# Moving VectorE's sums and additions in the doubled products of an encoder layer's second MLP half

## The chip, the cores and the metric

One of the eight cores of a Trainium2 chip runs the whole kernel in one launch. The metric is the device time of one execution in microseconds (us); the time of a kernel is the median of its runs.

## The reference, cut to what matters

The kernel computes one layer of an encoder on a sequence of 2048 positions with 1024 features, all in float32: an attention mixer with two groups of heads, and behind it an MLP with a squared ReLU. Everything of this case lies in the MLP:

```python
h = rmsnorm(x, g_norm2[l]) * (1.0 + sc2) + sh2
x = x + gt2 * (jnp.square(jax.nn.relu(h @ w1[l])) @ w2[l])
```

`w1` is 1024 x 4096, `w2` is 4096 x 1024, `gt2` is a gate per feature.

## The kernel before, in words

**Float32 from three passes.** Every operand of a matrix product is split into a rounded high part (a cast on ScalarE) and the rest (a subtraction on VectorE, 128 x 512 elements), and TensorE multiplies high by high, high by low and low by high (`mm3`). So each operand tile costs VectorE one subtraction, and the tiles that hold the split operands (`opp`, 8 buffers) bound how far the splitting can run ahead of TensorE.

**Fewer products, more sums.** A product of 2 x 2 blocks is done with seven products in place of eight, at the price of sums of blocks ahead of it and behind it (Strassen's scheme in Winograd's form). The seven are called 1, 5, 6, 3, 7, 2, 4, in the order of `OUTER`. `column_sum` is such a sum on VectorE.

**First half of the MLP** (`First`, h @ w1). It runs for two halves of the sequence, `mb` 1 and then `mb` 0. Each has 16 rows `j` (two column blocks of `w1`), and each row has seven steps, one for each product, of 12 matmuls. Row `j` needs three sums of blocks of `w1` in tiles of their own: `First.fetch` makes sum 5 (pieces 21 and 22), sum 6 (of sum 5 and piece 11), sum 3 (of piece 12 and sum 6) and, in place, sum 7. The tiles come from `temp`, a pool of 7 buffers of 128 x 512 (`tp`). In the profile they are `ts`: `ts<-w` is sum 5, `ts<-ts,w` sum 6, `ts<-w,ts` sum 3. In the half `mb` 0 the rows 0 to 7 also take four tiles each from this pool (`other`, in the profile `to`): a block of the hidden layer of `mb` 1, loaded, subtracted from on VectorE and stored to `scr_hid` by `keep`. Behind the products, `cp` in the profile holds the sums of results; the column sum behind product 7 reads the PSUM bank that product 4 of the same row goes on adding to.

**Second half of the MLP** (hidden @ w2). Products 1 and 6 are done plainly (`Second`, 16 steps of 24 matmuls each, `plain`). The other five, 7, 5, 2, 3, 4 in this order (`DOUBLE`), are each done once more by seven products (`Outer`), for both halves of the sequence at once: 56 steps of 6 matmuls, eight steps for each of 1, 5, 6, 3, 7, 2, 4. The order at the end of the kernel is: `First` of `mb` 0 (112 steps), `plain(0, 1)`, doubled 7, `plain(0, 6)`, doubled 5, 2, 3, 4.

A step of `Outer` uses an operand of the hidden layer (`opr` in the profile, one for each step) and one of the weights (`ol`, one for two steps). Ahead of that, VectorE makes, for each doubled product:

- sums of blocks of the hidden layer, 128 x 1024 elements, four (`g` 0 to 3) of each kind (`half_sum`, `r<-r,r` in the profile): 6 from 3 and 5, 7 from 6 and 1, 4 from 2 and 6, and for doubled product 5 alone also 5 from 5 and 1. `plan["sum"]` gives for each kind the step of the first and the gap to the next; it is made one doubled product ahead. `f` is the step at which the doubled product starts, `e` that at which it ends. A sum 6 is read from step 16 of its doubled product on, a sum 7 from step 32, a sum 4 from step 48, each some five steps earlier by the splitting.
- the loads of these blocks (`half`, at the steps of `plan["load"]`).
- behind the last step of 5, 6, 3, 7, 2 and 4 (steps 15, 23, 31, 39, 47, 55) the results, weighted by the gate and added to rows of x (`weigh`, `cxo` and `txo` in the profile): four for each of them in the doubled products 7 and 5, two in 2, 3 and 4.
- in 2, 3 and 4, `update`: four more rows added (`txu` in the profile), each fetched into a tile of `temp` at a step of its first list, added at a step of its second list, and stored three steps later.

The sums of blocks of `w2` for the doubled products are made beforehand, while `First` runs, and stored to `scr_t`. `outer_sums` does it in pieces of 128 x 2 x 256 (`wt` in the profile): a load into one of four large buffers (`raw_pair`, which also hold the rows of `w1`) six steps ahead, then four sums at four steps, each stored two steps later. `narrow_sums` does the same for half as much at a time, in two tiles of `temp` (`twn`): loads four steps ahead, four sums of 128 x 256 at four steps, each stored two steps later. Before, it serves doubled product 2 in `mb` 1 only.

**What sets the order.** Nearly everything here is written out by hand: `at(n, job)` puts a job at step n, and the loop over the steps prepares operands as far ahead as 8 buffers allow, then runs the jobs of the step, then its matmuls. Each engine, and the DMA queue of SyncE (SP), runs its instructions in exactly this order. A tile of a pool is taken by whoever asks next, and the writer waits until the last user of that buffer has finished (a store: until it has landed).

Of the kernel before, what the change touches and what calls it, by code (L numbers as in the profile page):

```python
# [9 lines left out]
F32 = mybir.dt.float32  # L10
# [8 lines left out]
P = 128  # L19
# [60 lines left out]
def encoder_kernel(ctx, tc, xT, c, g1, g2, w_in, w_rest, gqk, bias, w_o, w1, w2, w_ada, b_ada, out):  # L80
    nc = tc.nc
    act, dve, pool, sp = nc.scalar, nc.vector, nc.gpsimd, nc.sync
# [156 lines left out]
    if True:  # L239
# [248 lines left out]
        act, dve, pool = (Ordered(tc, e) for e in (act, dve, pool))  # L488
# [189 lines left out]
    if True:  # L678
# [540 lines left out]
        op = ph.enter_context(tc.tile_pool(name="op", bufs=2))  # L1219
# [69 lines left out]
    HP = NP // 2  # L1289
# [6 lines left out]
    if True:  # L1296
# [5 lines left out]
        np2 = pm.enter_context(tc.tile_pool(name="np2", bufs=2, side="right"))  # L1302
# [16 lines left out]
        def column_sum(eng, out, a, b, op):  # L1319
            eng.tensor_tensor(out, a, b, op=op)  # L1320
            return out

        def temp(nm):
            return tp.tile([P, TB], F32, tag="t", name=f"t{nm}")
# [9 lines left out]
        def at(n, job):  # L1334
            jobs.setdefault(n, []).append(job)
# [120 lines left out]
        class First(Step):  # L1456
# [29 lines left out]
            def fetch(self, m=None):  # L1486
                d = self.load()
                for n in range(4) if m is None else (m,):
                    pr, a, b, op = ((5, "21", "22", ALU.add), (6, 5, "11", ALU.subtract), (3, "12", 6, ALU.subtract), (7, "11", "21", ALU.subtract))[n]
                    d[pr] = column_sum(dve, d["21"] if pr == 7 else temp(f"s{self.nm}_{pr}"), d[a], d[b], op)  # L1490
                return d

            def run(self):
# [147 lines left out]
        def update(mb, r, odd, loads, adds, home=None, last=False):  # L1641

            xs = {}

            def fetch(n):
                xs[n] = x = (home or temp)(f"xu{mb}_{r}{odd}_{n}")
                sp.dma_start(x, scr_x[2 * mb + odd, HK * r + n])

            def add(n):
                x, row = xs[n], HK * r + n  # L1650
                weigh(x, Second.whole["s", n], row)
                dst = rows_of(out, mb, row, odd) if last else scr_x[2 * mb + odd, row]
                later.add(3, lambda: sp.dma_start(dst, x))

            for n in range(HK):
                at(loads[n], lambda n=n: fetch(n))
                at(adds[n], lambda n=n: add(n))
# [10 lines left out]
        def outer_sums(i, m, step):  # L1668

            t = []  # L1670

            def load():
                t.append(raw_pair([P, 2, 2, TB], F32, f"wt{i}_{m}"))
                for a in range(2):
                    if i in (3, 7, 5):
                        sp.dma_start(t[0][:, a], scr_s[i - 1 if i < 7 else 0, HP // 2 * a + m])
                        continue
                    r, s = {2: (0, 1), 4: (1, 1)}[i]
                    j = HP * a + 2 * m
                    for q in range(2):  # L1680
                        sp.dma_start(t[0][:, a, q, :], w2[2 * (j + q) + s][:, r * TB : (r + 1) * TB])

            def sums(pr, dst, a, b, op):
                v = {nm: t[0][:, h, :, c * CN : (c + 1) * CN] for nm, h, c in (("11", 0, 0), ("12", 1, 0), ("21", 0, 1), ("22", 1, 1))}
                column_sum(dve, v[dst], v[a], v[b], op)
                later.add(2, lambda: sp.dma_start(scr_t[i, pr][:, 2 * m : 2 * m + 2, :], v[dst]))

            at(step - 6, load)
            todo = ((5, "22", "21", "22", ALU.add), (7, "21", "11", "21", ALU.subtract))
            todo += ((6, "11", "22", "11", ALU.subtract), (3, "12", "12", "11", ALU.subtract))  # L1690
            for n, x in enumerate(todo):
                at(step + n, lambda x=x: sums(*x))

        def narrow_sums(i, k, step):

            t = []
            r, s = {2: (0, 1), 4: (1, 1)}[i]

            def load():
                for a in range(2):  # L1700
                    t.append(temp(f"wn{i}_{k}_{a}"))
                    sp.dma_start(t[a], w2[2 * (HP * a + k) + s][:, r * TB : (r + 1) * TB])

            def sums(pr, dst, a, b, op):
                v = {nm: t[h][:, c * CN : (c + 1) * CN] for nm, h, c in (("11", 0, 0), ("12", 1, 0), ("21", 0, 1), ("22", 1, 1))}
                column_sum(dve, v[dst], v[a], v[b], op)
                later.add(2, lambda: sp.dma_start(scr_t[i, pr][:, k, :], v[dst]))

            at(step - 4, load)
            todo = ((5, "22", "21", "22", ALU.add), (7, "21", "11", "21", ALU.subtract))  # L1710
            todo += ((6, "11", "22", "11", ALU.subtract), (3, "12", "12", "11", ALU.subtract))
            for n, x in enumerate(todo):
                at(step + n, lambda x=x: sums(*x))
# [154 lines left out]
        for mb in (1, 0):  # L1868
            begin = len(steps)
            steps += [First(mb, j, i) for j in range(NP) for i in OUTER]  # L1870
            end = len(steps)
            for j in range(NP):
                f = steps[begin + 7 * j]
                if mb:
                    second_sums(j, begin + 7 * j + 2)
                    if j >= HP:
                        narrow_sums(2, j - HP, begin + 71 + 5 * (j - HP))
                else:
                    outer_sums((7, 5, 3, 4)[j // 4], j % 4, begin + 7 * j - 2)
                    if j < HP:  # L1880
                        for i, n in ((3, 4), (2, 5), (7, 4), (4, 5)):
                            at(begin + 7 * j + n, lambda i=i, f=f: f.other(i))
                if j > mb:
                    at(begin + max(7 * j - 13, 2 if mb else -6), f.load)
                if j > mb or mb and j:
                    for m in range(4):
                        at(begin + (m + 1 if mb and j == 1 else 7 * j - 9 + (m if j > 1 else 0)), lambda f=f, m=m: f.fetch(m))
            if mb:
                norm2(1, begin + 18)
                norm2(0, begin + 48)  # L1890
                for k in range(HK):
                    begins = end + 6 * k
                    pieces = right_blocks(0, k, kept if k % 2 else temp)
                    for n, m in ((0, 0), (4, 4), (5, 5), (6, 6), (7, 7), (8, 7), (9, 7), (10, 7), (11, 7), (12, 7)):
                        at(begins + n, pieces[m])
                for i in PLAIN:
                    plain(1, i)
                for n in range(end, len(steps), 2):
                    at(n - 7 - max(0, end + 4 - n) // 2, steps[n].load)
                rest = len(steps)  # L1900
                lent = lambda nm: rp.tile([P, TB], F32, tag="r", name=nm)
                for n, (r, odd) in enumerate(((0, 0), (1, 1), (1, 0))):
                    at_row = rest + 3 + 16 * n
                    update(1, r, odd, range(at_row, at_row + 16, 4), range(at_row + 4, at_row + 20, 4), lent)
            else:
                at(begin - 8, steps[begin].load)
                at(begin - 6, steps[begin].fetch)
# [5 lines left out]
        f = plain(0, 1)  # L1913
        plain_loads(f, [9, 9, 9, 8, 8, 8])
        e = len(steps)
        plan = {"load": {1: (f - 3, 1), 5: (f + 1, 2), 3: (f + 6, 2), 2: (f + 18, 2)}}
        plan["sum"] = {6: (f + 12, 2), 7: (f + 15, 2), 4: (f + 44, 2)}
        for i in DOUBLE:
            f = outer(i, plan)
            e = len(steps)  # L1920
            if i == 7:
                plain_loads(plain(0, 6), [12, 11, 11, 11, 9, 8])
            spread = lambda *ns: [f + n for n in ns]
            if i == 2:
                update(0, 0, 0, spread(18, 22, 26, 30), spread(24, 28, 32, 36))
                pass
            if i == 3:
                update(0, 1, 1, spread(18, 22, 26, 30), spread(24, 28, 32, 36))
            if i == 4:
                update(0, 1, 0, spread(2, 6, 10, 14), spread(8, 12, 16, 20), None, True)  # L1930
            plan = {"load": {1: (f + 22, 2), 5: (f + 17, 2), 3: (f + 30, 2), 2: (f + 46, 2)}}
            plan["sum"] = {6: ({7: e + 8, 5: e - 4}.get(i, f + 38), 2), 7: (e + (20 if i == 7 else 16), 2), 4: (e + (30 if i == 7 else 26), 2)}
            if i == 7:
                plan["sum"][5] = (e + 1, 2)

        blocks = [right_blocks(1, k, kept if k else temp) for k in range(HK)]

# [104 lines left out]
```

## Time and profile before

| | |
|---|---|
| median of 3 runs | 2557.26 us (2556.21 to 2559.08) |
| the profiled execution's own time | 2558.36 us |
| its span, first to last instruction | 2556.6 us |
| granted TensorE clock | 0.999 |
| TensorE busy | 2520.1 us (99%) |
| TensorE weight loads busy | 2095.2 us (82%) |
| VectorE busy | 2055.6 us (80%) |
| ScalarE busy | 1510.6 us (59%) |
| DMA | 714.66 MB, mean 280 GB/s |

The matmuls are pipelined, so their durations overlap, and TensorE's busy time says little; what a step costs is read from the distance between the starts of two steps. In the rows of the timeline a bracket tells how long the engine stood idle before the instruction and what ended that. Idle time of VectorE or of SP costs nothing by itself; it counts where TensorE stands behind it.

### The profile page before, as it was taken

The page shows a single profiled execution, that of the slowest core. Times are in us where ns is not written, and L with a number is a line of the kernel's source. Part 1 is how long each engine was busy: PE and PEld are TensorE (multiplying, and loading weights), DVE is VectorE, ACT ScalarE, POOL GpSimd, SP SyncE. Part 2 cuts the span into 40 slices and gives each one's busy share as a digit, 9 for nine tenths or more (in the row PEclk, how much of TensorE's full clock was granted, in tenths as well). Part 3 has the DMA queues.
Part 4 walks back from the last instruction along what each step waited for, and adds up shares of the span by engine and source line. Part 5 has one row for each costly group of instructions (what it writes and reads, how often), then busy time and mean ns, then how long its engine had stood idle before and what let it go on. Part 6 is the DMA issues. An engine that isn't in the chain of part 4 may idle for free.

```text
span 2556.6 us, 39502 instructions
## 1 busy us (share of the span) xinstructions
PE 2520.1 (99%) x12388; PEld 2095.2 (82%) x12388; DVE 2055.6 (80%) x3593; ACT 1510.6 (59%) x2893; POOL 746.0 (29%) x1128
## 2 busy tenths in 40 slices
PE   9999999999999999999999999999999999999999
PEld 7888888888888888887888888888778888887777
DVE  7656767887789878998868777789887759899998
ACT  6333425668866687666755555575455546466665
POOL 4330144776776667776610000000000000000000
PEclk9999999999999999999999999999999999999999
DMA  9879979779977788866887888996998896868884
GB/s 360 327 294 365 342 279 295 213 237 287 285 238 235 236 253 272 262 211 194 233 312 251 296 288 311 336 344 220 339 338 289 273 354 264 339 240 292 284 261 130
DMA packets 305105, 714.66 MB, mean 280 GB/s; under 512 B 32512, under 2 KB 91904, under 8 KB 293248
## 3 DMA queue, kind: packets, MB, share of 16 engines
q1 hardware_dynamic: 303600, 707.43, 80.9%
q10 hardware_dynamic: 1296, 4.72, 0.5%
q8 instruction: 98, 1.61, 0.3%
q14 instruction: 111, 0.91, 0.1%
HBM read 485.00 MB, written 227.02 MB: 279 GB/s over the span
## 4 chain that ended last, share of the span: by engine, by line
PE 74%; DVE 14%; DMA 4%; ACT 3%; issue 3%; POOL 1%; SPq 0%; DVEq 0%; ACTq 0%; POOLq 0%
PE ps L42 21%; PE ps_s L42 11%; PE pt L42 11%; PE acc L42 6%; PE wt L42 6%; PE pf L42 4%; PE z L42 4%; PE po L42 4%; PE pq L42 3%; DVE opr L42 3%; DVE r L42 2%; DVE p L42 2%; PE cz L42 1%; DVE ol L42 1%; DVE txo L42 1%
## 5 line engine op out<-in xcount | busy, mean ns | idle before, releaser
L42 PE MATMUL ps<-h,opw 128*128 128x512 f32 x1512 | 358.6, 389 | 0.0
L42 ACT CAST wth<-wt 128x512 fp32r<-128x512 f32 (+3 forms) x544 | 257.3, 484 | 167.7 <-PE wt L42 158.0
L42 POOL TENSOR_TENSOR b<-p 128x512 f32<-128x512 f32 (+1 forms) x320 | 291.9, 912 | 168.9 <-DVE p L42 96.8
L42 DVE TENSOR_TENSOR wtl<-wt,wth 128x512 fp32r<-128x512 f32 (+3 forms) x544 | 291.2, 547 | 58.8 <-ACT wth L42 56.9
L42 PEld LDWEIGHTS ps<-h,opw 128*128 128x128 f32 x1512 | 283.7, 188 | 58.8
L42 PE MATMUL pt<-w,ht 128*128 128x512 f32 x1248 | 288.2, 391 | 0.0
L42 PE MATMUL ps_s<-h,opw 128*128 128x512 f32 x1152 | 278.1, 390 | 6.5 <-DVE cp L42 5.6
L42 PEld LDWEIGHTS pt<-w,ht 128*128 128x128 f32 x1248 | 233.0, 188 | 47.7
L42 DVE TENSOR_TENSOR_SCAN p<-z,p,zero 128x512 f32<-128x512 f32 x192 | 245.7, 1281 | 25.6 <-ACT z L42 18.3
L42 PEld LDWEIGHTS ps_s<-h,opw 128*128 128x128 f32 x1152 | 215.3, 188 | 54.5 <-DVE cp L42 8.3
L42 ACT CAST opr<-r 128x512 fp32r<-128x512 f32 x280 | 174.3, 623 | 142.5 <-PE ps L42 71.1
L42 PE MATMUL ps<-opr,ol 128*128 128x512 f32 x960 | 223.2, 391 | 1.5 <-DVE opr L42 1.2
L42 PE MATMUL acc<-wth,v 128*128 128x512 f32 (+3 forms) x544 | 221.0, 410 | 0.0
L42 PEld LDWEIGHTS ps<-opr,ol 128*128 128x128 f32 x960 | 179.4, 188 | 42.8 <-DVE opr L42 4.5
L42 DVE TENSOR_TENSOR opr<-r,opr 128x512 fp32r<-128x512 f32 x280 | 186.3, 691 | 16.2 <-ACT opr L42 14.8
L42 ACT ACTIVATE z<-z 128x512 f32<-128x512 f32 (+1 forms) x320 | 166.5, 520 | 55.4 <-PE z L42 49.0
L42 PE MATMUL z<-k,q 128*128 128x512 f32 (+3 forms) x640 | 185.6, 371 | 7.7 <-DVE p L42 7.0
L42 PE MATMUL acc<-wtl,v 128*128 128x512 f32 (+3 forms) x544 | 185.7, 348 | 0.0
L42 PE MATMUL ps<-oph,opv 128*128 128x512 f32 x768 | 176.0, 390 | 0.7 <-DVE oph L42 0.3
L42 PE MATMUL ps_s<-opr,ol 128*128 128x512 f32 x720 | 170.4, 392 | 3.7 <-DVE opr L42 3.3
L42 PE MATMUL wt<-ident,b 128*128 128x128 f32 x1088 | 171.3, 273 | 0.9 <-DVE p L42 0.6
L42 PEld LDWEIGHTS ps<-oph,opv 128*128 128x128 f32 x768 | 143.9, 188 | 32.3 <-DVE oph L42 1.2
(215 smaller groups left out, 4877.0 us busy)
## 6 DMA issues: line engine op xcount, KB each, us to landing
r<-scr_hid SPq DMA_DIRECT2D x80, 512.0 KB, 7.0
q<-scr_q SPq DMA_DIRECT2D x128, 256.0 KB, 5.2
w<-in_w_dram SPq DMA_DIRECT2D x64, 512.0 KB, 5.8
k<-scr_k SPq DMA_DIRECT2D x240, 128.0 KB, 4.5
v<-scr_v SPq DMA_DIRECT2D x120, 256.0 KB, 4.0
wa<-in_w_ada_dram SPq DMA_DIRECT2D x48, 512.0 KB, 6.4
ow<-scr_wo SPq DMA_DIRECT2D x24, 1024.0 KB, 6.0
l<-scr_t SPq DMA_DIRECT2D x20, 1024.0 KB, 7.2
```

The lines of the kernel that those rows point to most:

```text
L42: return lambda *x, **y: self.tc.keep_in_program_order(f(*x, **y))
```

## The change

- `First.fetch`: in `mb` 0 the tile of sum 5 comes from a buffer of its own (`np2`, tag `ndg`, one buffer of 128 x 512, used before by the norms) and no longer from `temp`.
- In `mb` 0 the sums of `w2` for the doubled products 7, 5 and 3 are made every 9 steps in place of every 7, and those for product 4 by `narrow_sums`, every 5 steps from step 65 on, in place of `outer_sums`.
- The half sums: kinds 6, 7 and 4 come four steps apart in place of two; their first ones are moved. In the doubled products 2, 3 and 4, counted from their own start: 6 from steps -18, -16, -14, -12 (product 2: -4, -2, 0, 2) to -4, 0, 4, 8; 7 from 16, 18, 20, 22 to 12, 16, 20, 24; 4 from 26, 28, 30, 32 to 28, 32, 36, 40. In product 5: 7 from 4, 6, 8, 10 to 12, 16, 20, 24; 4 from 14, 16, 18, 20 to 28, 32, 36, 40; 5 and 6 stay in `plain(0, 6)`. In product 7 only kind 4: from 28, 30, 32, 34 to 28, 32, 36, 40.
- The rows of `update`: fetched at steps 8, 16, 24, 32 and added at 14, 22, 30, 38 in all three; before, fetched at 18, 22, 26, 30 and added at 24, 28, 32, 36 (product 4: fetched at 2, 6, 10, 14, added at 8, 12, 16, 20).
- The loads of the next product's blocks of kind 1 are at steps 16, 20, 24, 28 in place of 22, 24, 26, 28.

```diff
                     pr, a, b, op = ((5, "21", "22", ALU.add), (6, 5, "11", ALU.subtract), (3, "12", 6, ALU.subtract), (7, "11", "21", ALU.subtract))[n]
-                    d[pr] = column_sum(dve, d["21"] if pr == 7 else temp(f"s{self.nm}_{pr}"), d[a], d[b], op)
+                    if pr == 7:
+                        t = d["21"]
+                    elif pr == 5 and not self.mb:
+                        t = np2.tile([P, 4, P], F32, tag="ndg", name=f"s{self.nm}_{pr}", bufs=1).rearrange("p a b -> p (a b)")
+                    else:
+                        t = temp(f"s{self.nm}_{pr}")
+                    d[pr] = column_sum(dve, t, d[a], d[b], op)
...
-                    outer_sums((7, 5, 3, 4)[j // 4], j % 4, begin + 7 * j - 2)
+                    if j < 12:
+                        outer_sums((7, 5, 3)[j // 4], j % 4, begin + 9 * j - 2)
                     if j < HP:
                         for i, n in ((3, 4), (2, 5), (7, 4), (4, 5)):
                             at(begin + 7 * j + n, lambda i=i, f=f: f.other(i))
+                    else:
+                        narrow_sums(4, j - HP, begin + 65 + 5 * (j - HP))
...
-        plan["sum"] = {6: (f + 12, 2), 7: (f + 15, 2), 4: (f + 44, 2)}
+        plan["sum"] = {6: (f + 12, 2), 7: (f + 15, 2), 4: (f + 44, 4)}
...
             if i == 2:
-                update(0, 0, 0, spread(18, 22, 26, 30), spread(24, 28, 32, 36))
+                update(0, 0, 0, spread(8, 16, 24, 32), spread(14, 22, 30, 38))
                 pass
             if i == 3:
-                update(0, 1, 1, spread(18, 22, 26, 30), spread(24, 28, 32, 36))
+                update(0, 1, 1, spread(8, 16, 24, 32), spread(14, 22, 30, 38))
             if i == 4:
-                update(0, 1, 0, spread(2, 6, 10, 14), spread(8, 12, 16, 20), None, True)
-            plan = {"load": {1: (f + 22, 2), 5: (f + 17, 2), 3: (f + 30, 2), 2: (f + 46, 2)}}
-            plan["sum"] = {6: ({7: e + 8, 5: e - 4}.get(i, f + 38), 2), 7: (e + (20 if i == 7 else 16), 2), 4: (e + (30 if i == 7 else 26), 2)}
+                update(0, 1, 0, spread(8, 16, 24, 32), spread(14, 22, 30, 38), None, True)
+            plan = {"load": {1: (f + 16, 4), 5: (f + 17, 2), 3: (f + 30, 2), 2: (f + 46, 2)}}
+            plan["sum"] = {6: (e - 4, 4), 7: (e + 12, 4), 4: (e + 28, 4)}
             if i == 7:
-                plan["sum"][5] = (e + 1, 2)
+                plan["sum"] = {5: (e + 1, 2), 6: (e + 8, 2), 7: (e + 28, 4), 4: (e + 44, 4)}
```

## The prediction

> **What bounds the kernel now.** I first read the busy times, then the stages by windows cut where TensorE's timeline changes its tiles.
>
> ```profile
> PE 2520.1 (99%) x12388; PEld 2095.2 (82%) x12388; DVE 2055.6 (80%) x3593; ACT 1510.6 (59%) x2893; POOL 746.0 (29%) x1128
> ```
>
> ```profile
> core 0: us, PE busy (x) PEld busy (x) DVE busy (x) ACT busy (x) POOL busy (x), PEclk, DMA share, GB/s
> 1758.90:2071.00 312.10, 306.42 (x1346) 251.74 (x1344) 240.35 (x383) 161.62 (x288) 0.00 (x0) 1.00 0.89 303
> 2071.00:2114.52 43.52, 43.52 (x194) 36.04 (x192) 25.89 (x39) 21.18 (x38) 0.00 (x0) 1.00 0.88 348
> 2114.52:2191.50 76.98, 76.88 (x337) 62.83 (x336) 75.06 (x114) 50.92 (x88) 0.00 (x0) 1.00 0.81 305
> 2191.50:2235.36 43.86, 43.82 (x193) 35.97 (x192) 35.49 (x51) 18.28 (x32) 0.00 (x0) 1.00 0.84 328
> 2235.36:2313.22 77.86, 77.14 (x337) 62.84 (x336) 76.20 (x117) 50.44 (x86) 0.00 (x0) 1.00 0.73 264
> 2313.22:2393.74 80.52, 78.74 (x337) 62.28 (x336) 79.33 (x117) 50.40 (x86) 0.00 (x0) 1.00 0.79 276
> 2393.74:2473.85 80.11, 78.35 (x338) 62.42 (x336) 75.75 (x113) 50.39 (x86) 0.00 (x0) 1.00 0.82 277
> 2473.85:2552.40 78.55, 77.75 (x337) 62.57 (x335) 69.35 (x105) 46.90 (x80) 0.00 (x0) 1.00 0.49 157
> ```
>
> These are `First` of `mb` 0, `plain(0, 1)`, doubled 7, `plain(0, 6)`, doubled 5, 2, 3 and 4: all that the change touches. The clock is full. TensorE sets the time, but not quite alone, as its timeline shows:
>
> ```profile
> start us, us, engine line op out<-in xcount [idle before <-releaser]
> 1848.91 2.88 PE L42 MATMUL ps<-h,opw 128*128 128x512 f32 x12
> 1853.30 3.01 PE L42 MATMUL ps_s<-h,opw 128*128 128x512 f32 x12 [1.51 <-DVE cp L42]
> ...
> 2114.52 21.92 PE L42 MATMUL ps<-opr,ol 128*128 128x512 f32 x96
> 2136.28 11.04 PE L42 MATMUL ps_s<-opr,ol 128*128 128x512 f32 x48
> ...
> 2366.91 4.16 PE L42 MATMUL ps_s<-opr,ol 128*128 128x512 f32 x17 [0.98 <-DVE opr L42]
> ...
> 2541.34 11.04 PE L42 MATMUL ps_s<-opr,ol 128*128 128x512 f32 x48
> ```
>
> Undisturbed, 96 matmuls (16 `Outer` steps) take 2136.28 - 2114.52 = 21.76 us: an `Outer` step 1.36 and 56 of them 76.16, a `First` step (12 matmuls) 2.72 and 112 of them 304.6, a plain product (192 matmuls) 43.52. So `First` lost 312.1 - 304.6 = **7.5 us**. The doubled products lost 0.8 (7), 1.7 (5), 4.4 (2), 3.95 (3) and, with 10.88 for the eight last steps from 2541.34, 2.2 (4); the plain ones 0 and 0.3. Together **20.8 us**, the most that the change can give.
>
> The brackets name VectorE both times, so the question is why VectorE is late.
>
> **First: the home for sum 5, and the sums every nine steps.**
>
> ```profile
> L42 DVE TENSOR_TENSOR ts<-w 128x512 f32<-128x512 f32 x15 | 10.3, 688 | 18.0 <-DMA scr_hid<-to 18.0
> ```
>
> ```profile
> 1816.19 0.69 DVE L42 TENSOR_TENSOR ts<-w 128x512 f32<-128x512 f32 x1 [1.75 <-DMA scr_hid<-to]
> 1837.62 0.69 DVE L42 TENSOR_TENSOR ts<-w 128x512 f32<-128x512 f32 x1 [3.28 <-DMA scr_hid<-to]
> 1840.09 0.69 DVE L42 TENSOR_TENSOR ts<-ts,w 128x512 f32<-128x512 f32 x1
> ...
> 1920.24 0.69 DVE L42 TENSOR_TENSOR ts<-w 128x512 f32<-128x512 f32 x1 [4.21 <-DMA scr_hid<-to]
> ```
>
> Sum 5 stands 18 us in all until a `to` tile has been stored: four `to` and three `ts` ask for seven buffers in each row, and the four `to` of the row before are still there. Everything of the row queues behind it on VectorE, `cp` too, and TensorE's product 4 waits for `cp`. A wait of 1.75 us puts no bracket on TensorE in its row; 3.28 cost 1853.30 - 1848.91 - 2.72 = 1.67. So a row hides about 1.7 us and the rest reaches TensorE.
>
> After: sum 5 waits for no store; its own buffer was last read by splitting, earlier in VectorE's own order, so I price its reuse at nothing (without that cover, one cast, 0.6 us). But the buffers are not plentiful: sum 6 now asks for the one that sum 5 waited for. It comes 1840.09 - 1837.62 = 2.5 us later, so the waits shrink to 3.28 - 2.5 = 0.8 and 4.21 - 2.5 = 1.7, inside what a row hides. The wider spacing also takes away two ninths of four sums of 0.6 us, some 0.5 us a row. I keep 0.6 us of the 7.5 (between 0 and 2.5, where the largest waits stay): **gain 6.9**.
>
> **The narrow pieces** replace 16 sums of 512 elements by 32 of 256, and 16 stores by 32, in rows 8 to 15, where no `to` is left. Their price is seen in `mb` 1, which does the same:
>
> ```profile
> L42 DVE TENSOR_TENSOR w2s<-w2s 128x512 f32<-128x512 f32 x25 | 17.2, 688 | 0.0
> L42 DVE TENSOR_TENSOR twn<-twn,twn 128x256 f32<-128x256 f32 x22 | 9.2, 420 | 0.0
> L42 DVE TENSOR_TENSOR ts<-ts,w 128x512 f32<-128x512 f32 x5 | 3.4, 686 | 1.5 <-DMA scr_t<-twn 1.5
> ```
>
> ```profile
> L42 PE MATMUL ps_s<-h,opw 128*128 128x512 f32 x504 | 121.6, 390 | 0.9 <-ACT cp L42 0.8
> ```
>
> VectorE: 32 x 0.42 - 16 x 0.69 = 2.4 us more over some 100 us, hidden, since a row without waits has slack (1.7 us above). Once a sum there waited 1.5 us for a narrow store, and TensorE idled 0.9 us in the whole of that half, none of it for this. I take 0; from below also 0, as the second half loses nothing there now; from above 1.5 us in each of five rows. [...] The transfers of that stretch of `mb` 1 (size, and median us to landing):
>
> ```profile
> w<-in_w_dram SPq DMA_DIRECT2D x8, 512.0 KB, 5.5
> ...
> scr_s<-w2s SPq DMA_DIRECT2D x16, 256.0 KB, 6.2
> ...
> scr_t<-twn SPq DMA_DIRECT2D x16, 128.0 KB, 5.6
> ```
>
> The half-size store lands 0.6 us sooner, so each tile comes free no later. [...]
>
> **The doubled products: sums and rows spread.** VectorE's pace there:
>
> ```profile
> 2338.01 1.22 DVE L42 TENSOR_TENSOR r<-r,r 128x1024 f32<-128x1024 f32 x1
> 2339.15 1.29 DVE L42 TENSOR_TENSOR opr<-r,opr 128x512 fp32r<-128x512 f32 x2
> 2340.35 0.69 DVE L42 TENSOR_TENSOR ol<-l,ol 128x512 fp32r<-128x512 f32 x1
> ...
> 2348.57 1.41 DVE L42 SCALAR_TENSOR_TENSOR txo<-ps_s,mod,txo 128x512 f32<-128x512 f32 x2
> 2349.89 0.69 DVE L42 TENSOR_TENSOR opr<-r,opr 128x512 fp32r<-128x512 f32 x1
> ```
>
> From start to start a half sum takes 1.14, a split 0.60, an added row 0.66. Eight steps (10.88) need twelve splits (7.24), which leaves **3.64 us** for the rest. In doubled 3 before, by steps: 8-15 two rows (1.32); 16-23 four sums, two rows (5.88); 24-31 three sums, four rows (6.06); 32-39 two sums, four rows (4.92); 40-47 three sums, two rows (4.74); 48-55 two rows. What exceeds 3.64 piles up: 2.24, 4.66, 5.94, **7.04**. The product lost 3.95, so the operands prepared ahead cover 3.1. The same for the others, peak and loss: product 2, 7.04 and 4.4 (cover 2.7); 5, with four rows behind each of its products, 4.84 and 1.7 (3.1); 4, 4.66 and 2.2 (2.45); 7, 2.62 and 0.8 (1.8). Five products give a cover of 1.8 to 3.1, mean 2.6: the excess explains the losses.
>
> After, in 3: steps 0-7 two sums (2.28); each of 8-15, 16-23, 24-31, 32-39 two sums and three rows (4.26, 0.62 too much); 40-47 and 48-55 one sum and two rows. Peak **2.48**, loss 0 (to 0.7 at the smallest cover); 4 alike. Product 5: 0.14, then 1.28 three times, then 0.14 twice: peak 4.26, loss 1.6 (1.1 to 2.5), and it hands a full backlog of 2.6 to product 2, which ends at 2.6 - 1.36 + 4 x 0.62 = 3.7: loss 1.1 (0.6 to 2.0). Product 7: the late peak falls to 1.5, loss 0.2. With 0.3 in `plain(0, 6)` and 0.2 each for 3 and 4, 3.6 us of 13.4 stay (1.7 to 6.6): **gain 9.7**.
>
> Nothing in it is late for its reader: the last sum 4 now comes at step 40 for a first use, at its first block, at 48, and its last block is read from 54 on; the last sum 6 at step 8 for 22. The `update` fetches move ahead of the loads of results at steps 9 and 11 on SP. If SP stands for a tile, the block and weight loads queue behind it; it does so today:
>
> ```profile
> SPq L42 <- DVE txo L42: 102.2, 33, 15.3
> ```
>
> Up to 15.3 us at once, without one wait of VectorE or TensorE for a load in that stretch; spaced eight steps, fewer `txu` tiles are held together, so I charge 0.
>
> **The rivals.**
>
> *A. VectorE's total is the bound there* (chance 0.06). The groups of doubled 3:
>
> ```profile
> L42 DVE TENSOR_TENSOR opr<-r,opr 128x512 fp32r<-128x512 f32 x56 | 37.3, 692 | 4.4 <-ACT opr L42 4.0
> L42 DVE TENSOR_TENSOR ol<-l,ol 128x512 fp32r<-128x512 f32 x29 | 20.1, 692 | 0.0
> L42 DVE TENSOR_TENSOR r<-r,r 128x1024 f32<-128x1024 f32 x12 | 14.7, 1223 | 0.0
> L42 DVE SCALAR_TENSOR_TENSOR txo<-ps_s,mod,txo 128x512 f32<-128x512 f32 x6 | 4.2, 755 | 0.0
> ```
>
> With full durations, 85 splits, 12 sums and 16 rows are 58.8 + 14.7 + 12.1 = 85.6 us against 76.16, and no order would help: only the 6.9 of the first stage comes, 2550.4. Against it: the product took 80.11, less than 85.6, and instructions start 0.60 apart; by that pace the need is 75.6, just under TensorE's 76.16, and VectorE even idled 4.4. [...]
>
> *B. The shortage only moves* (0.10): sum 6 stands at the store as long as sum 5 did. Then only the doubled products gain: 2557.3 - 9.7 = 2547.6. Against it is the 2.5 us between the two.
>
> *C. Slower* (0.07): two narrow tiles every five steps crowd the pool in rows 8 to 15, SP stands at their loads, the row of `w1` behind it comes late, and VectorE has nothing to split. It decides where SP stands longer than the lead, four steps (10.9 us), less the landing of a row of `w1` (5.5 above): 5.4 us. To end slower it must cost over 2 us at each of eight pieces; at 2.7, 21.6 - 16.6 = 5 more, 2562. Against it: `mb` 1 did it with sum 5 in the pool as well. [...]
>
> *D. Nothing measurable* (0.05): sums that a job list moves but VectorE runs as late as before; 2555.
>
> **How the numbers follow.** The forecast (0.72): 6.9 + 9.7 = 16.6 us. Against the profiled execution (2558.36): 2541.8; the median is 1.1 lower, so 2557.26 - 16.6 = **2541**. Its own ends are 16.6 + 3 (all but 1.2 of the loss gone) and 16.6 - 6.0 with every remainder at its bound, 2538 to 2547. The range must leave out no more than C and D: it reaches to A and B, 2537.5 to 2551. Faster by more than 0.2% (5 us, about what a measurement tells from no change): forecast, A and B, 0.88; within 0.05; slower 0.07.
>
> **What would show it.** Right: `ts<-w` waits for no store, TensorE's brackets `<-DVE cp` go, the stage of `First` takes 305 to 307; doubled 2, 3 and 4 take 76.2 to 77.3, 5 still over 77. Wrong: a wait of `ts<-ts,w` over 1.7 us in every row (B); VectorE without gaps through 2, 3 and 4 at 80 us each (A); TensorE waiting for `opw` or VectorE for `w<-in_w_dram` in rows 8 to 15 (C).

## The result, and the profile after

Four runs of the changed kernel have a median of 2545.3 us (2542.47 to 2545.75), four of the kernel before 2557.61; the ratio is 0.9952, interval 0.994 to 0.9965. It is faster, by 12.3 us by the medians where 16.6 were forecast. The profiled execution took 2545.14 us. (One execution of home_only and one of after_seven, two of the kernels below, took 12675 and 9169 us; the medians count them, the ratios do not.) The same stages as in the prediction, by windows (columns as there):

```profile
1755.69:2066.14 310.45, 307.07 (x1345) 253.18 (x1344) 241.28 (x399) 162.06 (x288) 0.00 (x0) 0.99 0.90 307
2066.14:2109.66 43.52, 43.52 (x193) 36.05 (x192) 25.89 (x39) 21.18 (x38) 0.00 (x0) 1.00 0.86 326
2109.66:2186.16 76.50, 76.50 (x338) 63.00 (x336) 74.77 (x114) 50.95 (x88) 0.00 (x0) 1.00 0.82 309
2186.16:2230.14 43.98, 43.81 (x193) 35.97 (x192) 35.61 (x51) 18.28 (x32) 0.00 (x0) 1.00 0.82 319
2230.14:2309.05 78.91, 78.07 (x338) 62.70 (x336) 75.16 (x115) 50.41 (x86) 0.00 (x0) 1.00 0.72 256
2309.05:2386.44 77.39, 76.99 (x338) 62.81 (x337) 77.39 (x117) 50.44 (x86) 0.00 (x0) 1.00 0.85 306
2386.44:2462.74 76.30, 76.30 (x337) 63.00 (x336) 75.10 (x113) 50.46 (x86) 0.00 (x0) 1.00 0.83 289
2462.74:2539.02 76.28, 76.28 (x337) 62.81 (x335) 71.00 (x107) 46.93 (x80) 0.00 (x0) 1.00 0.49 153
```

Less the undisturbed 304.64, 43.52 and 76.16, these stages lose 5.8, 0, 0.3, 0.5, 2.75, 1.2, 0.15 and 0.1: 10.85 us in place of 20.8. So 8.35 came from the doubled products and `plain(0, 6)`, and 1.65 from `First`. The first start also moved, 1758.90 to 1755.69. In four kernels that run the same program up to there (after, after_again, five_early, rows_before) it lies between 1755.7 and 1757.8, and in the others with these sums on VectorE between 1755.4 and 1758.9; so these 3.2 us are not put down to the change. The stages thus account for 10 of the 12.3 us; by after_again, further down, the gain by the medians is 9.6.

TensorE's timeline shows where the rest is lost, in row 6 of `First` and in the doubled products 5 and 2:

```profile
1883.76 2.88 PE L42 MATMUL ps<-h,opw 128*128 128x512 f32 x12
1889.56 4.57 PE L42 MATMUL ps_s<-h,opw 128*128 128x512 f32 x12 [2.92 <-DVE cp L42]
1893.97 4.26 PE L42 MATMUL ps<-h,opw 128*128 128x512 f32 x18
...
2282.05 4.15 PE L42 MATMUL ps_s<-opr,ol 128*128 128x512 f32 x17 [0.31 <-DVE opr L42]
...
2371.57 4.15 PE L42 MATMUL ps<-opr,ol 128*128 128x512 f32 x17 [0.29 <-DVE opr L42]
```

In `First` the four brackets of 1.25 to 1.51 us are gone, and one twice as long stands in row 6. VectorE's groups of that stage name what it stood at (`s<-w` is now sum 5, `ts<-s,w` sum 6):

```profile
L42 DVE TENSOR_TENSOR s<-w 128x512 f32<-128x512 f32 x15 | 10.3, 688 | 3.3 <-DMA w<-in_w_dram 3.2
L42 DVE TENSOR_TENSOR ts<-s,w 128x512 f32<-128x512 f32 x15 | 10.3, 686 | 3.9 <-DMA scr_hid<-to 3.8
L42 DVE TENSOR_TENSOR ts<-w,ts 128x512 f32<-128x512 f32 x15 | 10.3, 686 | 3.8 <-DMA scr_t<-twn 3.8
```

Sum 5 waits for no store any more, but 3.2 us in all for loads of `w1`; sum 6 waits 3.8 us for a store, and sum 3 once for a narrow store. VectorE's and SP's timelines at that row, and the landing of the `to` transfers around it:

```profile
1874.47 0.69 DVE L42 TENSOR_TENSOR ts<-s,w 128x512 f32<-128x512 f32 x1 [3.82 <-DMA scr_hid<-to]
```

```profile
1860.26 1.00 SPq L42 DMA_DIRECT2D w<-in_w_dram  x2
...
1862.31 1.29 SPq L42 DMA_DIRECT2D wt<-scr_s  x2
1863.64 0.94 SPq L42 DMA_DIRECT2D scr_x<-xu  x1
1864.69 1.38 SPq L42 DMA_DIRECT2D scr_hid<-to  x2
```

```profile
DMA to landing us min/median/max: 4.6/5.2/9.1
```

Four big loads, two of a row of `w1` and two of the spread sums, are issued just ahead of the `to` stores. The first `to` store, issued at 1864.69, is the one that takes 9.1 us to land; the second, issued at 1865.75, takes 8.6, and sum 6 starts 0.1 us after it has landed.

### The profile page after: what moved, and what is told of

Read it like the earlier page. It is cut to its first block, busy times and chain, and to the rows that moved or that the text cites. A ratio compares the mean times of both kernels' runs of the same rounds, so it can differ in the third digit from the quotient of the medians.

```text
span 2543.4 us, 39545 instructions
## 1 busy us (share of the span) xinstructions
PE 2513.3 (99%) x12388; PEld 2095.6 (82%) x12388; DVE 2053.9 (81%) x3609; ACT 1510.3 (59%) x2893; POOL 746.0 (29%) x1128
## 4 chain that ended last, share of the span: by engine, by line
PE 80%; DVE 10%; ACT 4%; issue 3%; DMA 3%; POOL 1%; SPq 0%; DVEq 0%; POOLq 0%; ACTq 0%
PE ps L42 24%; PE ps_s L42 14%; PE pt L42 11%; PE acc L42 6%; PE wt L42 6%; PE pf L42 4%; PE z L42 4%; PE po L42 4%; PE pq L42 3%; DVE opr L42 2%; DVE p L42 2%; PE cz L42 1%; DVE ol L42 1%; PE ct L42 1%; DVE r L42 1%
## 5 line engine op out<-in xcount | busy, mean ns | idle before, releaser
L42 PEld LDWEIGHTS wt<-ident,b 128*128 128x128 f32 x1088 | 136.4, 140 | 41.4 <-DVE wtl L42 1.7
```

What stands on the lines that cost most here:

```text
L42: return lambda *x, **y: self.tc.keep_in_program_order(f(*x, **y))
```

## The experiments

What each kernel's profiled execution loses in each stage, in us, worked out as above; `plain(0, 1)` loses nothing in any of them. The last column is the ratio to the kernel before on the same chip, with its interval; medians of kernels from different chips are not to be compared closely, as the kernel before itself lies between 2555.2 and 2557.6.

| kernel | First | d7 | plain 6 | d5 | d2 | d3 | d4 | all | median us | ratio |
|---|---|---|---|---|---|---|---|---|---|---|
| before | 7.5 | 0.8 | 0.3 | 1.7 | 4.4 | 3.95 | 2.2 | 20.8 | 2557.6 | |
| after | 5.8 | 0.3 | 0.5 | 2.75 | 1.2 | 0.15 | 0.1 | 10.85 | 2545.3 | 0.9952 [0.994, 0.9965] |
| home_only | 5.7 | 0.8 | 0.35 | 1.7 | 4.3 | 3.9 | 2.2 | 19.1 | 2554.65 | 0.9991 [0.9982, 1.0] |
| doubled_only | 6.4 | 0.3 | 0.5 | 2.75 | 1.2 | 0.1 | 0.1 | 11.5 | 2548.18 | 0.9968 [0.9956, 0.998] |
| after_seven | 6.5 | 0.3 | 0.5 | 2.75 | 1.2 | 0.1 | 0.1 | 11.5 | 2546.67 | 0.9957 [0.9944, 0.997] |
| after_no_narrow | 5.5 | 0.3 | 0.5 | 2.75 | 1.2 | 0.1 | 0.1 | 10.5 | 2544.47 | 0.9954 [0.9942, 0.9965] |
| home_light | 13.5 | 0.3 | 0.5 | 2.75 | 1.2 | 0.1 | 0.1 | 18.5 | 2553.42 | 0.9989 [0.9979, 0.9999] |
| after_again | 5.6 | 0.3 | 0.5 | 2.75 | 1.2 | 0.1 | 0.1 | 10.6 | 2546.27 | 0.9963 [0.995, 0.9977] |
| pool_sums | 6.65 | 0.3 | 0.5 | 2.75 | 1.2 | 0.1 | 0.1 | 11.7 | 2553.81 | 0.9991 [0.9982, 1.0] |
| five_early | 6.95 | 0.3 | 0.5 | 0 | 0.1 | 0.1 | 0.1 | 8.1 | 2542.75 | 0.9946 [0.9933, 0.996] |
| five_phase | 2.3 | 0.3 | 0.5 | 0 | 0.1 | 0.1 | 0.1 | 3.5 | 2543.4 | 0.9944 [0.9932, 0.9957] |
| five_xu | 4.85 | 0.3 | 0.5 | 0 | 0.1 | 0.15 | 0.1 | 6.0 | 2542.32 | 0.9944 [0.9931, 0.9958] |
| rows_before | 1.8 | 0.3 | 0.5 | 2.75 | 1.2 | 0.2 | 0.05 | 6.9 | 2542.89 | 0.9946 [0.9928, 0.9964] |
| late_sums | 0.04 | 0.3 | 0.55 | 0 | 0.1 | 0.1 | 0.1 | 1.3 | 2536.97 | 0.9926 [0.9913, 0.994] |

`First` is the same program in after, after_again, five_early and rows_before, and loses 5.8, 5.6, 6.95 and 1.8 there. So a difference of a few us in that column between two kernels proves nothing by itself. Sum 6 waits in row 6 in all four, 3.8, 4.55, 4.8 and 2.6 us; the wait belongs to the kernel, its length to the execution. The other columns repeat within 0.2 us.

### home_only: the kernel before, with only the home for sum 5

```diff
+                    elif pr == 5 and not self.mb:
+                        t = np2.tile([P, 4, P], F32, tag="ndg", ...)
```

> The kernel before with the own buffer for sum 5 alone. Theory 1 (what stayed lost in the first stage after the change comes from the nine-step spacing, whose loads drift against the seven-step rows and once land ahead of the stores that free the tiles): the first stage loses under 1.5 us of the 7.5, the wait of sum 6 for a store stays under 1.7 us in every row, the time is 2551 to 2552. Rival (the seven buffers are still too few whatever the spacing): the first stage still loses 4 to 6 us, 2554.5 to 2556.

The ratio's interval ends at 1.0, and `First` loses 5.7 us: the rival's outcome, not theory 1's. VectorE's timeline at two of the sums 6, its group of the sums 5, and TensorE's timeline in the same rows:

```profile
1854.95 0.69 DVE L42 TENSOR_TENSOR ts<-s,w 128x512 f32<-128x512 f32 x1 [1.87 <-issue]
...
1896.29 0.69 DVE L42 TENSOR_TENSOR ts<-s,w 128x512 f32<-128x512 f32 x1 [2.24 <-issue]
```

```profile
L42 DVE TENSOR_TENSOR s<-w 128x512 f32<-128x512 f32 x15 | 10.3, 687 | 6.1 <-DMA w<-in_w_dram 6.1
```

```profile
1869.11 3.01 PE L42 MATMUL ps_s<-h,opw 128*128 128x512 f32 x12 [1.16 <-DVE cp L42]
1909.68 4.54 PE L42 MATMUL ps_s<-h,opw 128*128 128x512 f32 x12 [1.87 <-DVE cp L42]
```

Four sums 6 in a row stand 1.9, 1.5, 2.2 and 1.9 us. The profile names no releaser for them ("issue"), but each starts 0.08 us after a `to` store has landed: the one issued at 1848.52, for instance, takes 6.35 us to land, and the sum 6 starts at 1854.95. In the kernel before, the sums 5 of these rows stood 1.6, 3.2, 3.0 and 4.2. The waits for stores have moved and shrunk by 1.1 us in the mean, not by 2.5. And sum 5, free of the stores, now stands for the load of its row of `w1`, 0.7, 1.6, 1.1 and 0.95 us in these four rows. Both waits together are 11.7 us against 12.1 before: VectorE stands about as long as it did, in two places.

### doubled_only: the changed kernel without the home, the spacing and the narrow pieces

```diff
-                    if pr == 7: ... elif pr == 5 and not self.mb: ...
+                    d[pr] = column_sum(dve, d["21"] if pr == 7 else temp(f"s{self.nm}_{pr}"), d[a], d[b], op)
...
+                    outer_sums((7, 5, 3, 4)[j // 4], j % 4, begin + 7 * j - 2)
```

> The change without its part in the first stage: only the half sums, the rows and the loads of the doubled products are moved. By the ledger of VectorE's excess: the first stage loses 7.5 us as before, the doubled products and the plain one between them 5.0 (0.3, 0.5, 2.75, 1.2, 0.15, 0.1) in place of 13.4, the time is 8.4 lower, 2549.2. Rival (the doubled products gain because the first stage hands over less late work): they lose over 8 us, 2552 or more.

Ratio 0.9968: most of the change's gain. The doubled products lose what they lose in the whole change; the two parts do not touch each other there.

### after_seven and after_no_narrow: the spacing and the narrow pieces alone

```diff
-                        outer_sums((7, 5, 3)[j // 4], j % 4, begin + 9 * j - 2)
+                        outer_sums((7, 5, 3)[j // 4], j % 4, begin + 7 * j - 2)
```

> The changed kernel with the sums for the doubled products 7, 5 and 3 every seven steps again (twelve of them), all else as changed. Theory 1 (drift of the nine-step spacing): the first stage loses under 1.5 us in place of 5.8, 2541. Rival (too few buffers whatever the spacing): 4 to 6 us stay lost, 2544 to 2546; if the wider spacing helped, 6 to 8 stay lost and the time is 2546 to 2548.

```diff
-                    if j < 12:
-                        outer_sums((7, 5, 3)[j // 4], j % 4, begin + 9 * j - 2)
...
-                    else:
-                        narrow_sums(4, j - HP, begin + 65 + 5 * (j - HP))
+                    outer_sums((7, 5, 3, 4)[j // 4], j % 4, begin + 7 * j - 2)
```

> The changed kernel with all sixteen sums every seven steps in large buffers, no narrow pieces: sum 5 has its own buffer and the doubled products are spread. Theory 1: first stage under 1.5 us lost as with the own buffer alone, 2541. If the narrow pieces matter by freeing large buffers: 2 to 4 us more lost than with twelve sums every seven steps and the narrow pieces.

0.9957 and 0.9954 beside 0.9952: neither the narrow pieces (between these two) nor the nine steps (after_seven against after) make a difference that these runs can tell. In after_seven the sums 6 stand 1.5, 2.55, 2.2 and 1.5 us in rows 5 to 8, as in home_only. The explanation that only the drift of the nine steps brings the loads onto the stores fell with it.

### home_light: the changed kernel with lighter transfers for the spread sums

```diff
-                        sp.dma_start(t[0][:, a], scr_s[..., HP // 2 * a + m])
+                        sp.dma_start(t[0][:, a, :, 0:CN], scr_s[..., HP // 2 * a + m][:, :, 0:CN])
...
-                later.add(2, lambda: sp.dma_start(scr_t[i, pr][:, 2 * m : 2 * m + 2, :], v[dst]))
+                later.add(2, lambda: sp.dma_start(scr_d[i, pr][:, 2 * m : 2 * m + 1, 0 : CN // 2], v[dst][:, 0:1, 0 : CN // 2]))
```

> The changed kernel with less to move for the nine-step sums: each of their loads brings half the bytes and each of their stores a quarter of the half (to a place that nobody reads), with as many transfers and sums as before; the sums of doubled products 7, 5 and 3 are therefore not computed. Theory 3 (the amount that the DMA engines move in rows 0 to 8 sets when the stores of the to tiles land, and so when sum 6 gets its tile): these stores land after under 5.5 us at the median in place of 7.1, no wait of sum 6 over 0.5 us, the first stage loses under 1 us of 5.8. Rival (what VectorE has to do, or where SP stands, sets it): landings may be shorter, but a wait over 1.5 us and over 3 us of loss stay.

`First` lost 13.5 us, more than any other kernel, because the edit made a wait of its own: the four sums now work on the same half of the tile, so each waits for the store of the last one. The waits of VectorE, and TensorE's largest bracket:

```profile
DVE wt L42 <- DMA scr_d<-wt: 12.1, 5, 7.6
```

```profile
1973.27 5.49 PE L42 MATMUL ps_s<-h,opw 128*128 128x512 f32 x12 [4.92 <-DVE cp L42]
```

That decides nothing on time. What it does show: over rows 0 to 7, with the DMA engines' share at 0.78 in place of 0.91 and VectorE's busy time as in the changed kernel (131.84 and 132.17 us), sum 6 stood at no store. The waits at `wt` delay VectorE too, 1.8 us of them between 1800 and 1925, so the fewer bytes are not the only difference.

### after_again and pool_sums: is it VectorE's load?

after_again is the changed kernel once more, on the chip of the next two.

> The changed kernel once more. If the one wait of 3.8 us of sum 6 in row 6 belongs to the kernel (its nine-step loads against its seven-step rows), it is there again in the same row, with 5 to 6 us lost in the first stage; if it is a matter of the single execution, it is in another row or none, and the loss differs by over 2 us. The doubled products lose 0.3, 2.75, 1.2, 0.15 and 0.1 again. 2545.

Ratio 0.9963, the same row, sum 6 standing 4.55 us: the wait in row 6 is the kernel's, not an accident of one execution. What it costs is not fixed: 5.8 and 5.6 us were lost here, 1.8 in rows_before. pool_sums puts the spread sums on GpSimd:

```diff
-                column_sum(dve, v[dst], v[a], v[b], op)
+                column_sum(pool, v[dst], v[a], v[b], op)
```

> The changed kernel with the nine-step sums on GpSimd, which idles in this half of the kernel, in place of VectorE. Rival theory (VectorE's own load in rows 0 to 8 is what leaves no slack): with 2 us a row less to do the first stage loses under 1 us, 2541. Theory 3 (stores land late): sum 6 still waits as often and as long, the added slack takes up about 2 us of the longest wait, 2 to 4 us of 5.8 stay lost, 2543. If GpSimd slows VectorE, or its slower sums hold the large buffers, over 6 us are lost.

Giving the 48 sums to GpSimd gained nothing: 0.9991, the change's gain gone. `First` itself lost only 0.9 us more than in the changed kernel; most of the rest lies ahead of it, where GpSimd makes its first four sums and TensorE stands 1.81 us for an operand, and `First` starts at 1760.8, later than in any other kernel. The groups of GpSimd and VectorE in `First`, and both timelines over one burst of four sums:

```profile
L42 POOL TENSOR_TENSOR wt<-wt 128x512 f32<-128x512 f32 x44 | 68.1, 1547 | 213.8 <-DMA wt<-scr_s 101.0 <-DMA scr_t<-wt 70.4 <-issue 28.0
...
L42 DVE TENSOR_TENSOR opw<-s,opw 128x512 fp32r<-128x512 f32 x16 | 14.2, 888 | 0.0
```

```profile
1828.76 6.71 POOL L42 TENSOR_TENSOR wt<-wt 128x512 f32<-128x512 f32 x4 [20.66 <-DMA wt<-scr_s]
```

```profile
1829.14 1.78 DVE L42 SCALAR_TENSOR_TENSOR xu<-cs,mod,xu 128x512 f32<-128x512 f32 x1
1830.84 1.78 DVE L42 TENSOR_TENSOR to<-cz,to 128x512 f32<-128x512 f32 x1
1832.54 1.77 DVE L42 TENSOR_TENSOR opw<-ts,opw 128x512 fp32r<-128x512 f32 x1
```

While GpSimd works, these VectorE instructions, whose operands all lie in SBUF, take 1.78 us and not 0.69 (0.75 for the first kind); they start 1.70 us apart, and GpSimd's four sums take 6.71, 1.68 each. Those that read one operand from PSUM do not slow: three that start beside GpSimd's sums between 1800 and 1900 us take 0.68 each, and over the whole stage the groups `cp<-ps,cp`, `cp<-ps_s,cp` and `cs<-ps,cs` have means of 684, 684 and 680 ns. So VectorE's load was not lightened, and the run cannot decide the question in the heading.

### five_early: the doubled product's own term

```diff
-                plan["sum"] = {5: (e + 1, 2), 6: (e + 8, 2), 7: (e + 28, 4), 4: (e + 44, 4)}
+                plan["sum"] = {5: (e + 1, 2), 6: (e + 8, 2), 7: (e + 9, 2), 4: (e + 18, 8)}
```

This makes sums 7 and 4 of doubled product 5 earlier, sums 7 already in `plain(0, 6)`, where VectorE is busy 35.6 of 44 us.

> The changed kernel with the sums of doubled product 5 moved: kind 7 into the plain product ahead (its steps 9, 11, 13, 15), kind 4 to the steps 2, 10, 18, 26 of product 5. By the ledger of VectorE's excess the peak in product 5 falls from 4.26 to 0.42 us and nothing is handed to product 2: product 5 loses under 0.5 us in place of 2.75, product 2 under 0.4 in place of 1.2, the plain product stays under 0.8; 3 us less, 2542. Rival (product 5 loses because TensorE waits for something that the ledger does not hold, results or loads): 2 us or more stay lost.

The windows of the doubled products 5 and 2:

```profile
2232.13:2308.29 76.16, 76.16 (x338) 63.08 (x336) 72.88 (x114) 50.46 (x86) 0.00 (x0) 1.00 0.76 272
2308.29:2384.58 76.29, 76.29 (x337) 63.01 (x336) 76.29 (x115) 50.45 (x86) 0.00 (x0) 1.00 0.85 301
```

5 is undisturbed, and with no backlog handed on 2 loses 0.1 in place of 1.2, although VectorE is busy all of its 76.29 us. A VectorE that is busy all the time costs nothing here while it is not behind. The 3.9 us in the stages are 2.75 + 1.2; by the medians beside after_again it is 3.5.

### five_phase and five_xu: other ways out of row 6

Both have five_early's line. five_phase moves one piece by four steps; five_xu takes the tiles of `xu`, rows of x that are added during `First`, from the twelve-buffer pool `kept`, not from a pool of two (`rp`).

```diff
+                        outer_sums((7, 5, 3)[j // 4], j % 4, begin + 9 * j - 2 + (4 if j == 5 else 0))
```

> The changed kernel with the sums of doubled product 5 moved (as in the run before) and with one of the nine-step loads, the sixth, and its sums four steps later, so that its two half-megabytes stand behind the stores of the to tiles of row 5 in SP's order and no longer ahead of them. Theory 4 (these loads ahead of the stores are what makes sum 6 of row 6 wait 3.8 to 4.8 us): that wait falls under 1.5 us, steps 47 and 48 lose under 1 us in place of 4.8 to 6.3, the first stage loses 1 to 2 us, 2538. Rival (the sheer amount moved in these rows, or VectorE's load, sets it): the wait comes in the next row or stays, 5 us or more stay lost, 2542.5.

```diff
-                lent = lambda nm: rp.tile([P, TB], F32, tag="r", name=nm)
+                lent = kept
```

> The changed kernel with the sums of doubled product 5 moved and the twelve rows that are added during rows 0 to 8 of the first stage (xu) in the pool of twelve tiles in place of two lent ones, so that SP does not stand until the store of an earlier row has landed. Theory 5 (SP stands there up to 4.8 us, and what queues behind it comes in a burst with the stores): the wait of sum 6 in row 6 falls under 1.5 us, the first stage loses under 2 us, 2538. Rival (theory 4, the nine-step load ahead of the stores): the wait stays over 2.5 us, 5 us or more lost, 2542.5.

In five_phase the stall of row 6 is gone (sum 6 waits 1.1 us there, 1.3 in row 7) and a smaller one, 1.55 us, stands in row 7: which transfers stand ahead of the `to` stores does move the wait. Its `First` lost 2.3 us, yet its median is no better than five_early's (0.9944 and 0.9946): the profiled execution, 2540.2 us, was the fastest of its five. In five_xu sum 6 stands 0.3 us only, but now ScalarE stands for a tile of the crowded pool and a row 3 stall appears (ScalarE's and TensorE's timelines):

```profile
1828.17 0.58 ACT L42 COPY cp<-ps_s 128x512 f32<-128x512 f32 x1 [5.53 <-DMA scr_hid<-ca]
```

```profile
1828.81 4.62 PE L42 MATMUL ps_s<-h,opw 128*128 128x512 f32 x12 [2.13 <-ACT cp L42]
```

As at sum 5, the user that gets room hands the wait to another one. Neither kernel came near the 2538 that was expected of it.

### rows_before: the changed kernel with the rows of `update` where they were

```diff
-                update(0, 0, 0, spread(8, 16, 24, 32), spread(14, 22, 30, 38))
+                update(0, 0, 0, spread(18, 22, 26, 30), spread(24, 28, 32, 36))
```

(the lists of doubled 3 and 4 likewise)

> The changed kernel with the rows of the updates in doubled products 2, 3 and 4 fetched and added at the steps of before; the half sums stay spread. By the ledger of VectorE's excess the peak in product 3 is 2.56 us in place of 2.48, in 4 2.56, so the spread of the rows alone is worth nothing: products 3 and 4 lose under 0.4 us each, 2 under 1.5. Rival (the rows' spread carries part of the gain): products 2, 3 and 4 lose over 1 us more each.

The windows of doubled 3 and 4:

```profile
2384.55:2460.94 76.39, 76.39 (x337) 62.99 (x336) 75.16 (x113) 50.47 (x86) 0.00 (x0) 1.00 0.82 288
2460.94:2537.16 76.22, 76.22 (x337) 62.82 (x335) 70.92 (x107) 46.90 (x80) 0.00 (x0) 1.00 0.50 155
```

0.2 and 0.05 us lost. Spreading the rows is worth nothing that shows; the spread of the sums did it, with the loads of kind 1, which no run moves alone.

### late_sums: fewer of the sums while `to` is alive

```diff
+                        outer_sums((7, 5, 3)[j // 4], j % 4, begin + (14 * j if j < 4 else 7 * j + 28) - 2)
```

With five_early's line; the steps of rows 0 to 7 take up five pieces in place of seven, the rest comes behind them.

> The changed kernel with the sums of doubled product 5 moved and the large sums of the first stage laid out anew: four of them every fourteen steps in rows 0 to 7, where the to tiles are, the other eight every seven steps in rows 8 to 15, beside the narrow pieces. Theory 3 (the amount moved in rows 0 to 8 sets when the stores of the to tiles land): with 38 us for each two megabytes in place of 24.5 these stores land sooner, sum 6 waits under 1 us in every row to 8, and the first stage loses under 1 us in rows 0 to 8; 2538. Rival (one transfer ahead of the stores, not the amount): sum 6 still waits over 2 us in a row where a load stands ahead of the stores. Against both: rows 8 to 15 now carry twice as many sums beside the narrow pieces, and what is won comes back as waits for narrow stores, 3 us or more lost there.

The windows of `First` and of its rows 0 to 7, then two groups of VectorE in `First`:

```profile
1757.89:2062.57 304.68, 304.68 (x1346) 252.18 (x1344) 241.29 (x399) 162.68 (x288) 0.00 (x0) 1.00 0.91 310
1757.89:1910.25 152.36, 152.36 (x674) 126.05 (x672) 125.90 (x202) 81.49 (x145) 0.00 (x0) 1.00 0.88 295
```

```profile
L42 DVE TENSOR_TENSOR ts<-s,w 128x512 f32<-128x512 f32 x15 | 10.3, 685 | 0.0
...
L42 DVE TENSOR_TENSOR ts<-w,ts 128x512 f32<-128x512 f32 x15 | 10.3, 684 | 0.0
```

Neither sum 6 nor sum 3 waits, and `First` loses nothing: 304.68. (Sum 5 still waits 3.7 us for loads of `w1`, in rows 11 to 14 and without cost to TensorE.) In the changed kernel rows 0 to 7 were:

```profile
1755.69:1913.03 157.34, 154.42 (x673) 127.11 (x672) 132.17 (x212) 81.00 (x145) 0.00 (x0) 0.99 0.91 311
```

For the same rows the bytes moved fall from 48.9 to 44.9 MB (GB/s times length), and VectorE's busy time by 6.3 us, with ten sums fewer. So the run cannot tell less to move from less for VectorE to do; the landing of the `to` stores does not settle it either, with a median of 6.3 us here, 7.1 in the changed kernel, but 6.5 in rows_before, which runs the changed `First`. Median 2536.97 (2536.23 to 2537.91): the fastest kernel of this case, ratio 0.9926, 18.3 us below the kernel before. All five runs lie below every run of the changed kernel.

## Why the prediction was right, and where it was off

The time lies inside the range, on the side that was forecast, 4.3 us above the forecast. It is even inside the forecast's own ends, 2538 to 2547, but that is in part luck: one of the two gains held and the other did not, the stages gained 10 us and not 16.6, and some 2 us of the 12.3 by the medians come from outside them. The 2547.6 of rival B is nearer to the measured time than the forecast's 2541. Step by step:

**The doubled products: right but for one term.** Doubled 7, 2, 3 and 4 were forecast to keep 0.2, 1.1, 0.2 and 0.2 us, and kept 0.3, 1.2, 0.15 and 0.1. The ledger's reason held too: without product 5's backlog product 2 loses 0.1 (five_early). (By the ledger the 1.1 of product 2, 2.48 - 1.36, comes out whatever the cover is, as long as product 5 hands on a full backlog.) Rival A, VectorE's total as the bound, is out: TensorE lost 0.1 in a product in which VectorE had no gap. A term was mis-sized: product 5 was to keep 1.6 (1.1 to 2.5) and kept 2.75, more than the 1.7 it lost before the change. With the peak of 4.26 that is a cover of 1.5, less than the 1.8 to 3.1 read from the products of the kernel before. Cover is not one constant; what sets it in a product was not tried.

**First: the step that failed** is "so the waits shrink to 3.28 - 2.5 = 0.8 and 4.21 - 2.5 = 1.7, inside what a row hides". It gave a gain of 6.9 us; 1.65 were measured (1.75 in home_only). The sign that was named for it, a stage of 305 to 307 us without brackets `<-DVE cp`, did not come either. Three things were wrong in it.

1. The wait at the store did not shrink by the distance: by 1.1 us in the mean in home_only, where sum 5 then stood for loads of `w1` instead, a wait that the prediction does not price. The four `to` tiles still come free only when their stores land, and a row that lost less before arrives sooner at the next store (this last is a reading of the rows). That is rival B's mechanism. Its test, a wait over 1.7 us in every row, was too strict: the whole wait sits in one row in the changed kernel and in four in home_only.

2. What a row hides is not a constant 1.7 us, read from one row. The other rows of the kernel before hide 1.3 to 2.7 us by the starts of TensorE's steps; row 6 of the changed `First` hides 0.7, 1.2, 0.03 and 1.4 in its four executions (3.82 us of wait, for instance, reach TensorE as 3.08).

3. The longer wait cost more than its length, which the prediction's price left out. These are the windows around the bracket of 2.92 us in the changed kernel:

```profile
1884.00:1889.50 5.50, 2.64 (x12) 1.86 (x10) 5.50 (x10) 1.73 (x4) 0.00 (x0) 1.00 0.95 298
1889.50:1894.00 4.50, 4.44 (x13) 3.58 (x14) 3.34 (x6) 2.19 (x5) 0.00 (x0) 0.62 1.08 362
1894.00:1897.00 3.00, 3.00 (x15) 2.47 (x14) 1.18 (x2) 1.71 (x4) 0.00 (x0) 1.00 1.03 381
```

Behind the stall the granted clock is 0.62: the step of product 4 takes 1893.97 - 1889.56 = 4.41 us and not 2.72. So row 6 cost 3.1 us by waiting and 1.7 by the clock, of the 5.8 that `First` lost. doubled_only has a stall of 1.59 us (TensorE's timeline, and the window of its step):

```profile
1852.74 3.06 PE L42 MATMUL ps_s<-h,opw 128*128 128x512 f32 x12 [1.59 <-DVE cp L42]
```

```profile
1852.70:1855.60 2.90, 2.86 (x12) 2.36 (x13) 1.29 (x2) 2.78 (x6) 0.00 (x0) 1.00 1.05 360
```

There the clock stays at 1.00. The change put one stall behind which the clock fell in the place of four behind which it did not, each of which had cost about 0.3 us more than its length. That is one part of why it gained so little in `First` although VectorE's waits for `to` stores fell from 18.0 us at sum 5 to 3.8 at sum 6. In rows_before, the same `First`, sum 6 waited 2.6 us, TensorE stood 1.06, the clock did not fall, and 1.8 us were lost.

**The spacing and the narrow pieces** were priced at some 0.5 us a row gained and 0. Neither shows in the times. Rival C did not come: sum 3 waited once for a narrow store, 2.6 to 3.75 us in row 11 of seven of the kernels, which cost TensorE 0.1 to 1.0. Moving the `update` rows neither gained nor lost anything that shows (rows_before).

**What stays open.** late_sums changes three things in rows 0 to 7 at once: the bytes in the queue, the use of the large buffers and VectorE's sums. home_light speaks for the bytes and five_phase for the order of the transfers, but neither isolates one cleanly, and no run lightens VectorE alone. Also open is why the same `First` loses 1.8 us in one execution and 5.6 to 6.95 in three others.

## What to carry to other kernels

Where one in-order engine is nearly as busy as TensorE, keep a ledger for each stretch of its work against the slack: here the loss was the peak of the backlog less what was prepared ahead, within 0.2 us in four products of five, and spreading work whose readers come late was free. Look at what is issued ahead of a store whose landing frees a tile: here one issued just behind four big loads took 9.1 us to land, where the median was 5.2. A private buffer handed the wait to the next asker, while moving sums, with their loads and stores, out of that stretch removed it. Look at the largest single stall as well as the sum: per us of idling the long one cost more here (4.8 us for 2.9) than a short one (1.8 for 1.5).

## What the runs showed of the hardware

The clock's step was not expected. From 1700 us on, where matmuls of 128x512 follow each other densely, the kernel before has six idle times of TensorE over 0.7 us, 0.97 to 1.51; behind all of them the matmuls follow 0.34 us apart once and then 0.22 to 0.24, the clock stays at 1.00, and the next 14 take 0.13 to 0.17 us more than undisturbed. Behind 0.84 us in home_light, 1.06 in rows_before, 1.16 in home_only, 1.55 in five_phase and 1.59 in doubled_only the group of 12 takes 3.01 to 3.06 us, against 2.88 undisturbed. Longer idle times, with the matmuls behind them and the mean granted clock over a window that holds them (14 matmuls undisturbed are estimated from the 2.88 of 12 and 0.227 for each more):

| kernel, TensorE idle us | matmuls behind it, us (undisturbed) | granted clock, over us |
|---|---|---|
| pool_sums 1.81 | 14 in 6.17 (3.3) | - |
| home_only 1.87 | 12 in 4.54 (2.88) | 0.63 over 4.40 |
| after_seven 2.03 | 12 in 4.61 (2.88) | 0.62 over 4.50 |
| five_xu 2.13 | 12 in 4.62 (2.88) | 0.99 over 125 |
| after 2.92 | 12 in 4.57 (2.88) | 0.62 over 4.50 |
| after_again 3.2 | - | 0.64 over 4.30 |
| five_early 4.60 | 12 in 4.41 (2.88) | - |
| home_light 4.92 | 12 in 5.49 (2.88) | 0.98 over 318 |

The four windows of 4.3 to 4.5 us, which lie close around those matmuls, have 0.62 to 0.64. The stretch of the changed kernel, by its window:

```profile
1889.49:1892.90 3.41, 3.34 (x8) 2.70 (x9) 3.08 (x6) 2.20 (x5) 0.00 (x0) 0.50 1.09 342
```

So the clock fell behind 1.87 us of idling in home_only and stayed at 1.00 behind 1.59 us in doubled_only.

The length alone does not tell it, though. Far ahead of these stages, among smaller matmuls and in a part of the program that is the same in all these kernels, TensorE stands 1.04 us before 616.79 in the kernel before and 1.05 us before 616.83 in the changed one. The windows behind these two (before, after):

```profile
618.24:621.65 3.41, 3.41 (x16) 3.31 (x16) 2.65 (x12) 2.57 (x7) 2.08 (x4) 0.50 0.99 286
618.20:621.60 3.40, 3.40 (x27) 3.28 (x26) 2.69 (x14) 3.24 (x9) 2.29 (x4) 1.00 0.95 288
```

The clock fell to 0.50 for 3.41 us behind this idle time in the one execution and stayed at 1.00 in the other. So something else decides with it; what that is was not tried.

GpSimd's sums took 1547 ns each in pool_sums, and VectorE's instructions beside them, where all their operands lie in SBUF, up to 1.79 us in place of 0.69. So VectorE was busier in `First` with 48 instructions fewer (246.88 us against 241.28).
